# A transformer layer: the shift sums of the first products on 128 columns with idle products behind them, the first block by k-tiles, mixer casts behind the decays, and steps of the ada queue in last units

## The chip, the core and the metric

The kernel runs on one core of a Trainium2 chip. The core has TensorE (PE: products of matrices, into the banks of PSUM), VectorE (DVE), ScalarE (ACT), GpSimd (POOL) and SyncE (SP), which work through queues of their own and wait for each other by semaphores. DMA queues move data between HBM and the on-chip memory, SBUF; in this kernel SP and POOL issue them, each in its own order. The metric is the time of one execution on the device, in microseconds (us), and the median of several runs.

## The reference

One layer on 256 tokens of width 2048, in fp32, with a conditioning vector c:

```python
ada = (silu(c) @ w_ada + b_ada)
sh1, sc1, g1, sh2, sc2, g2, sh3, sc3, g3 = split(ada, 9)
modulate(x, sh, sc) = layernorm(x) * (1 + sc) + sh
h = (silu(gate) * up) @ ffn1_w_out,  gate, up = split(modulate(x, sh1, sc1) @ ffn1_w_in)
x = layernorm(ALPHA * x + 0.5 * (1 + g1) * h, ln1_g, ln1_b)
h = token_mixer(modulate(x, sh2, sc2), w_in, ...)       # 8 fox attention heads, 4 mLSTM heads
x = layernorm(ALPHA * x + (1 + g2) * h, ln2_g, ln2_b)
h = second FFN on modulate(x, sh3, sc3)
x = layernorm(ALPHA * x + 0.5 * (1 + g3) * h, ln3_g, ln3_b)
```

w_ada is 2048 x 18432, the FFN's hidden width 5632, w_in has the columns of fox q, k, v and forget gates and of mLSTM q, k, v, gates and o. So nearly all bytes are weights that are read once, and each weight meets 256 tokens.

## The kernel before

**Products.** Each fp32 product is made of three products in fp32r: a weight or a row is split into a rounded part hi (a cast, on ACT, line 150) and a rest lo (a subtraction, on DVE, line 151), and `mm3` (lines 399 to 401) adds hi x hi, lo x hi and hi x lo in PSUM. `load_w` (line 374, or 378 in parts) issues one weight unit of 1 MB on SP, into three raw buffers, and splits it in pieces of 128x1024 into six hi and six lo buffers; its argument `behind` names an instruction behind which these splits stand in the order of ACT and DVE. The order of instructions within each engine is otherwise the order in which the code issues them, with the pieces marked `pinned` or `manual_schedule` held where they are written.

**The ada vector.** `silu(c) @ w_ada` isn't made on PE but on DVE: slices of 128 rows x 1024 columns (0.5 MB) are multiplied by a column of csil and summed over k into an accumulator (lines 163 and 165). At the end of 16 slices the 128 partitions are summed by PE with a matrix of ones (`bc`, line 178, one product with ahi and one with alo), and for shifts and scales the diagonal is taken on DVE (lines 195 and 197) into `scsh`, one column per 128 features. `AdaQueue` holds these units for the whole layer: `pump(n)`, called once in each weight unit of a stage, runs a step of a finished unit's tail (casts, bc, diagonal) and then as many slices as are owed; `need(n)` runs what is missing until n units are done, and sets the debt `owed` to zero. The accumulators and slices have the names `acc`, `gate`, `ar`. In the last four units of an output's last group (`out_proj`) pump isn't called.

**The start.** Only the shifts and scales of the first 512 features (block j = 0) are needed for the first products. `first_ada0` loads the 16 slices from SP. The half of a slice that holds the scales is summed on DVE (into `gate`), the half with the shifts on PE: the `row` products (line 824), one csil column times 512 columns, into one partition of PSUM. After the sixteenth, ACT copies the row to SBUF (`shifts`, line 828), and for each k-tile of 128 features `first_columns` turns the shifts (line 789) and the scales (line 787) into columns with one-column products and adds the bias (DVE, line 791, `scsh`). `modulate_both` then writes x of that tile: ACT makes xf (line 325) and its cast xhi_f (line 328), DVE the rest xlo_f (line 331). `first_in(j, i)` makes block i of twelve for the 512 features j: 48 products of 256 columns into two PSUM tiles, all four k-tiles for one half of the columns (h = 0), then for the other; for j = 0 ACT copies the sums to `hT1a` or `hT1b` (line 894), and later rounds add to them. Between blocks `next(fa)` runs slices of the next features' sums (issued from POOL, line 850), as many as a table says.

**The mixer.** `form_a_four` makes four heads' columns of q or k (m0 and m1 for the mLSTM heads, fb and fbk for q and k of fox heads 4 to 7, then fa and fak for 0 to 3) from four weight units of 48 products each; `step()` after each unit runs work of the heads. A part of `mlstm_head`, which runs in the units of fb and fbk, is the decay of the head: PE makes gb and the two scores sps (lines 1301 and 1303), ACT Relu and Exp of the decay (lines 1306 and 1307, into `dm`), DVE masks it and multiplies it with the scores (lines 1308 and 1309). One part of the scores lies in a PSUM tile of which there is one, so the next head's scores wait until DVE has read it.

## Time and profile before

| | us |
|---|---|
| median of 3 runs | 1929.29 |
| their spread | 1928.31 to 1930.26 |
| the profiled execution | 1927.28 |
| its span | 1925.6 |
| PE busy | 1891.5 (98%) |
| DVE busy | 1483.4 (77%) |
| ACT busy | 953.7 (50%) |
| POOL busy | 59.7 (3%) |
| DMA queue of SP, share of 16 engines | 73.4% |
| DMA queue of POOL | 4.4% |

The span is what the profile shows from the first instruction to the last; the execution's own time is 1.7 longer. A row of a timeline has the start in us, the time in us, the engine, the line, the operation, out<-in, the shape, the count, and in brackets how long the engine sat idle before it and what ended that. PE's product of 256 columns is listed with its latency (0.28 us and more), and products follow each other more closely than that; an fp32 product gives two records. The granted clock is 1.00 at full rate.

### The profile page before, as it was taken

What the parts mean: (1) busy time and instruction counts of PE and PEld (TensorE: products, weight loads), DVE (VectorE), ACT (ScalarE), POOL (GpSimd) and SP (SyncE); (2) the same over time, 40 slices, a digit from 0 to 9 for tenths busy, and PEclk for the clock granted to TensorE, in tenths of its full rate; (3) what the DMA queues carried; (4) which work ended last, traced back from release to release, by engine and by line L of the source; (5) the groups of instructions that cost most, each with busy time, mean ns of one, the idle gap of its engine ahead of it and who ended that gap; (6) DMA issues with size and microseconds to landing.
All of it is one profiled execution on the core that took longest, in us unless ns stands there. A gap on an engine that the chain in (4) does not pass through costs nothing.

```text
span 1925.6 us, 32413 instructions
## 1 busy us (share of the span) xinstructions
PE 1891.5 (98%) x13133; PEld 1724.6 (90%) x13133; DVE 1483.4 (77%) x1847; ACT 953.7 (50%) x1359; POOL 59.7 (3%) x88
## 2 busy tenths in 40 slices
PE   6999999999999999999999999999999999999997
PEld 3999999999988887699989886999999999988886
...
GB/s 359 375 262 313 328 218 296 337 331 306 266 339 296 267 301 236 138 321 317 319 300 272 315 300 114 338 282 246 262 248 260 246 213 196 240 184 189 196 196 89
DMA packets 283662, 510.92 MB, mean 265 GB/s; under 512 B 10962, under 2 KB 134514, under 8 KB 282488
## 3 DMA queue, kind: packets, MB, share of 16 engines
q1 hardware_dynamic: 275640, 480.53, 73.4%
...
## 4 chain that ended last, share of the span: by engine, by line
PE 84%; DVE 7%; DMA 5%; issue 2%; ACT 1%; SPq 0%; DVEq 0%; POOL 0%; ACTq 0%
PE gu_f L401 8%; PE gu_f L400 8%; PE gu_f L399 8%; PE o_f L399 6%; PE o_f L401 6%; PE o_f L400 6%; PE s L400 4%; PE s L399 4%; PE s L401 4%; DMA ar<-in_w_ada_dram 3%; PE fs L401 1%; PE fs L399 1%; PE fs L400 1%; PE o_mx L399 1%; PE o_mx L401 1%
## 5 line engine op out<-in xcount | busy, mean ns | idle before, releaser
L165 DVE SCALAR_TENSOR_TENSOR acc<-ar,csil,acc 128x1024 f32<-128x1024 f32 (+1 forms) x167 | 211.4, 1267 | 52.2 <-DMA ar<-in_w_ada_dram 51.5
L400 PE MATMUL s<-xlo_f,hi_s 128*128 128x256 f32 x768 | 213.6, 278 | 1.2 <-DVE xlo_f L331 1.2
L399 PE MATMUL s<-xhi_f,hi_s 128*128 128x256 f32 x768 | 213.4, 279 | 0.0
L401 PE MATMUL s<-xhi_f,lo_s 128*128 128x256 f32 x768 | 213.3, 278 | 0.0
L401 PE MATMUL gu_f<-xhi_f,lo_f2i 128*128 128x256 f32 x768 | 212.0, 276 | 0.0
L399 PE MATMUL gu_f<-xhi_f,hi_f2i 128*128 128x256 f32 x768 | 212.0, 276 | 0.0
L400 PE MATMUL gu_f<-xlo_f,hi_f2i 128*128 128x256 f32 x768 | 212.0, 276 | 0.0
L151 DVE TENSOR_TENSOR lo_f2i<-raw_f2i,hi_f2i 128x1024 fp32r<-128x1024 f32 x96 | 117.4, 1224 | 92.4 <-ACT hi_f2i L150 92.4
L401 PE MATMUL gu_f<-xhi_f,lo_f1i 128*128 128x256 f32 x640 | 176.7, 276 | 0.0
L399 PE MATMUL gu_f<-xhi_f,hi_f1i 128*128 128x256 f32 x640 | 176.7, 276 | 0.0
L400 PE MATMUL gu_f<-xlo_f,hi_f1i 128*128 128x256 f32 x640 | 176.7, 276 | 0.0
L150 ACT CAST hi_f2i<-raw_f2i 128x1024 fp32r<-128x1024 f32 x96 | 100.8, 1050 | 135.4 <-PE gu_f L400 124.6
L150 ACT CAST hi_s<-raw_s 128x1024 fp32r<-128x1024 f32 x96 | 100.6, 1052 | 130.3 <-PE s L400 93.4
L400 PEld LDWEIGHTS s<-xlo_f,hi_s 128*128 128x128 f32 x768 | 145.5, 189 | 1.5 <-DVE xlo_f L331 1.5
L401 PEld LDWEIGHTS s<-xhi_f,lo_s 128*128 128x128 f32 x768 | 145.4, 189 | 0.0
L399 PEld LDWEIGHTS s<-xhi_f,hi_s 128*128 128x128 f32 x768 | 144.9, 189 | 0.0
L399 PEld LDWEIGHTS gu_f<-xhi_f,hi_f2i 128*128 128x128 f32 x768 | 144.2, 188 | 0.2
L400 PEld LDWEIGHTS gu_f<-xlo_f,hi_f2i 128*128 128x128 f32 x768 | 144.2, 188 | 0.2
L401 PEld LDWEIGHTS gu_f<-xhi_f,lo_f2i 128*128 128x128 f32 x768 | 144.2, 188 | 0.0
L151 DVE TENSOR_TENSOR lo_f2o<-raw_f2o,hi_f2o 128x1024 fp32r<-128x1024 f32 x86 | 105.2, 1223 | 43.3 <-ACT hi_f2o L150 43.3
L165 DVE SCALAR_TENSOR_TENSOR gate<-ar,csil,gate 128x1024 f32<-128x1024 f32 (+1 forms) x94 | 117.5, 1251 | 25.4 <-DMA ar<-in_w_ada_dram 25.2
L151 DVE TENSOR_TENSOR lo_s<-raw_s,hi_s 128x1024 fp32r<-128x1024 f32 x96 | 115.5, 1219 | 27.4 <-ACT hi_s L150 27.2
...
## 6 DMA issues: line engine op xcount, KB each, us to landing
ar<-in_w_ada_dram SPq DMA_DIRECT2D x227, 512.0 KB, 5.4
...
```

The lines of the kernel that those rows point to most:

```text
L150: S.copy(hi, src)
L151: return V.tensor_tensor(out=lo, in0=src, in1=hi.bitcast(F32), op=ALU.subtract)
L165: V.scalar_tensor_tensor(out=acc, in0=raw, scalar=csil[:, k:k + 1], in1=acc, op0=ALU.mult, op1=ALU.add)
L399: PE.matmul(o, ah, bh, start=start, stop=False)
L400: PE.matmul(o, ah, bl, start=False, stop=False)
L401: PE.matmul(o, al, bh, start=False, stop=stop)
```

## The change

It has six parts.

1. The `row` products take the csil column broadcast to 128 columns, so that the sum of the shifts stands in all 128 partitions of PSUM. The bias of the shifts is added there by four products of an identity column with the bias rows (`load_bcol(part)`, called at the fifth slice). In `columns0` DVE takes the diagonal of 128x128 out of PSUM into scsh; the copy of the row and the four products of the shifts are gone.
2. Idle products (128x256, fp32r, into a PSUM tile that nobody reads) are put behind rows 10 to 14 (3, 3, 3, 12, 3) and behind the first two column products (2, 2).
3. Block (0, 0) goes by k-tiles: for each k-tile both halves of the columns.
4. The first three slices of the next features (j = 1) are issued from SP, between raw_s_1 and raw_s_2, instead of from POOL, and the table of steps behind blocks 0 and 1 of j = 0 is 0, 3 instead of 2, 1; for j = 0 the casts of block i stand behind the copies of block i - 3. The three gbias loads go from SP to POOL.
5. In `form_a_four` the splits of a weight unit stand behind the Exp of a head's decay (`decays`).
6. The tail step of `pump` is a method of its own, `end_step`, which is also called in the last four units of an output's last group and behind the last two calls of `half_in` in the second FFN.

On PE, at the end of the first ada sums, stood before (row_150 is the PSUM row, gate and shifts the sums, cp and cq the columns, s_0_0 the first block's PSUM tile):

```order
L824 MATMUL row_150<-ar_0_13_214,csil 1x512
L824 MATMUL row_150<-ar_0_14_224,csil 1x512
L824 MATMUL row_150<-hT1a,csil 1x512
L789 MATMUL cp_235<-trir,shifts 128x1
L787 MATMUL cp_235<-trir,gate 128x1
L789 MATMUL cq_236<-trir,shifts 128x1
L787 MATMUL cq_236<-trir,gate 128x1
L789 MATMUL cp_235<-trir,shifts 128x1
L787 MATMUL cp_235<-trir,gate 128x1
L789 MATMUL cq_236<-trir,shifts 128x1
L787 MATMUL cq_236<-trir,gate 128x1
L399 MATMUL s_0_0_267<-xhi_f_124,hi_s_00_220 128x256
```

and stands now (row_150 is now 128 partitions, idle_151 the tile that nobody reads):

```order
L858 MATMUL row_150<-ar_0_13_227,csil 128x512
L845 MATMUL idle_151<-trir 128x256 x12
L858 MATMUL row_150<-ar_0_14_249,csil 128x512
L845 MATMUL idle_151<-trir 128x256 x3
L858 MATMUL row_150<-hT1a,csil 128x512
L816 MATMUL cp_262<-trir,gate 128x1
L845 MATMUL idle_151<-trir 128x256 x2
L816 MATMUL cq_263<-trir,gate 128x1
L845 MATMUL idle_151<-trir 128x256 x2
L816 MATMUL cp_262<-trir,gate 128x1
L816 MATMUL cq_263<-trir,gate 128x1
L405 MATMUL s_0_0_299<-xhi_f_124,hi_s_00_245 128x256
```

The four products of `shifts` are gone, and idle products stand between the rows and the columns.

On ACT, in the mixer at the change from unit group fb to fbk, where head 0's gb and the scores are made (dm is the decay of an mLSTM head, hi_fbk a weight piece's rounded part, qs the scaled q of a fox head), stood before:

```order
L150 CAST hi_fbk_10448<-raw_fbk_10446 128x1024
L150 CAST hi_fbk_10476<-raw_fbk_10446 128x1024
L150 CAST hi_fbk_10540<-raw_fbk_10538 128x1024
L150 CAST hi_fbk_10568<-raw_fbk_10538 128x1024
L1306 ACTIVATE dm_10354<-gb_10352,nacol 128x256
L1306 ACTIVATE dm_10354<-gb_10352,nacol 128x128
L1307 ACTIVATE dm_10354<-dm_10354 128x256
L1307 ACTIVATE dm_10354<-dm_10354 128x128
L150 CAST hi_fbk_10621<-raw_fbk_10619 128x1024
L1383 ACTIVATE qs_10711<-pr_fb_10121 128x256
L150 CAST hi_fbk_10649<-raw_fbk_10619 128x1024
```

and stands now:

```order
L1355 ACTIVATE dm_10398<-gb_10396,nacol 128x256
L1355 ACTIVATE dm_10398<-gb_10396,nacol 128x128
L1356 ACTIVATE dm_10398<-dm_10398 128x256
L1356 ACTIVATE dm_10398<-dm_10398 128x128
L153 CAST hi_fbk_10489<-raw_fbk_10487 128x1024
L153 CAST hi_fbk_10517<-raw_fbk_10487 128x1024
L1432 ACTIVATE qs_10752<-pr_fb_10172 128x256
L1355 ACTIVATE dm_10473<-gb_10471,nacol 128x256
L1355 ACTIVATE dm_10473<-gb_10471,nacol 128x128
L1356 ACTIVATE dm_10473<-dm_10473 128x256
L1356 ACTIVATE dm_10473<-dm_10473 128x128
L153 CAST hi_fbk_10581<-raw_fbk_10579 128x1024
```

The decay of each head (first 10398, then 10473) moved ahead of the casts of one unit, and the casts of the second unit stand behind the second head's decay.

On PE the column sums bc_3_1 of the ada queue stood before inside the second FFN's gate products (gf), with products between the one with ahi and the one with alo:

```order
L400 MATMUL gf_13839<-lo_gu_13846,xhi_f_12456 128x512
L178 MATMUL bc_3_1_13828<-ahi_3_1_13824,trir 128x512
L401 MATMUL gf_13839<-hi_gu_13845,xlo_f_12457 128x512
L399 MATMUL gf_13840<-hi_gu_13845,xhi_f_12456 128x512
L400 MATMUL gf_13840<-lo_gu_13846,xhi_f_12456 128x512
L401 MATMUL gf_13840<-hi_gu_13845,xlo_f_12457 128x512
L399 MATMUL gf_13841<-hi_gu_13845,xhi_f_12456 128x512
L400 MATMUL gf_13841<-lo_gu_13846,xhi_f_12456 128x512
L401 MATMUL gf_13841<-hi_gu_13845,xlo_f_12457 128x512
L178 MATMUL bc_3_1_13828<-alo_3_1_13825,trir 128x512
```

They stand now as a pair inside the products of fh. At the end of the mixer's output (o_mx), where no column sums stood before, there are now those of bc_2_0 and bc_2_1; yw and hi_mxo are weight pieces, y the mixer's rows:

```order
L407 MATMUL o_mx_12181<-hi_mxo_01_12306,ylo 128x512
L181 MATMUL bc_2_0_12353<-ahi_2_0_12296,trir 128x512
L181 MATMUL bc_2_0_12353<-alo_2_0_12297,trir 128x512
L405 MATMUL o_mx_12336<-yw,yh_11433 128x512
L406 MATMUL o_mx_12336<-yw_12339,yh_11433 128x512
L407 MATMUL o_mx_12336<-yw,yl_11434 128x512
L405 MATMUL o_mx_12336<-yw,yh_11433 128x512
L406 MATMUL o_mx_12336<-yw_12340,yh_11433 128x512
L407 MATMUL o_mx_12336<-yw,yl_11434 128x512
L181 MATMUL bc_2_1_12387<-ahi_2_1_12359,trir 128x512
```

The pair of bc_2_1 is pulled apart there as that of bc_3_1 was in gf: its product with alo_2_1 follows twelve products behind the one with ahi_2_1.

The diff:

```diff
@@ -108,3 +108,3 @@
-    def load_bcol():
+    def load_bcol(part):
         brow = ap.tile([72, 2, P], F32, tag="ahi", name="brow")
@@ -114,2 +114,5 @@
             PE.transpose(bps[:, i * 72:(i + 1) * 72], brow[:, i, :], ident[:72, :72])
+        for q in range(4):
+            PE.matmul(part[:, q * P:(q + 1) * P], ident[:72, q:q + 1].to_broadcast([72, P]), brow[:, 0, :],
+                      start=False, stop=False)
         V.tensor_copy(bcol.rearrange("p v k -> p (v k)"), bps[:, :144])
@@ -126,5 +129,5 @@
         SP.dma_start(hrow[5:6, :], mlstm_norm_g)
-        SP.dma_start(gbias[:, 0:8], fox_f_bias[0:1, :].to_broadcast([P, 8]))
-        SP.dma_start(gbias[:, 8:12], mlstm_i_bias[0:1, :].to_broadcast([P, 4]))
-        SP.dma_start(gbias[:, 12:16], mlstm_f_bias[0:1, :].to_broadcast([P, 4]))
+        G_.dma_start(gbias[:, 0:8], fox_f_bias[0:1, :].to_broadcast([P, 8]))
+        G_.dma_start(gbias[:, 8:12], mlstm_i_bias[0:1, :].to_broadcast([P, 4]))
+        G_.dma_start(gbias[:, 12:16], mlstm_f_bias[0:1, :].to_broadcast([P, 4]))
         yield
@@ -251,7 +254,10 @@
+        def end_step(self):
+            if self.tails:
+                with pinned():
+                    self.tail()
+
         def pump(self, n):
             self.owed += n
-            with pinned():
-                if self.tails:
-                    self.tail()
+            self.end_step()
             while self.owed >= 1:
@@ -527,2 +533,4 @@
                     npump()
+                else:
+                    ada.end_step()
             if lastg:
...
@@ -806,2 +808,29 @@
+    def columns0(acc, part, mb, ws, idle):
+        cps = aux_tile("cp0"), mm_tile("cq0")
+        diag = ap.tile([P, 2, 512], F32, tag="acc", name="diag0")[:, 0, :P]
+
+        def column(q, n):
+            cp = cps[q % 2][:, q:q + 1]
+            qs = slice(q * P, (q + 1) * P)
+            mm = PE.matmul(cp, acc[:, qs], ones[:, 0:1], start=True, stop=True)
+            idle(n, mm)
+            V.scalar_tensor_tensor(out=diag, in0=part[:, qs], scalar=1.0, in1=ident, op0=ALU.mult, op1=ALU.mult,
+                                   accum_out=scsh[:, 0, q:q + 1])
+            V.tensor_tensor(out=scsh[:, 1, q:q + 1], in0=cp, in1=bcol[:, 1, q:q + 1], op=ALU.add)
+
+        column(0, 2)
+        next(mb)
+        column(1, 2)
+        next(mb)
+        next(mb)
+        column(2, 0)
+        next(mb)
+        column(3, 0)
+        next(ws)
+        next(mb)
+        for _ in mb:
+            pass
+
+
@@ -810,4 +839,9 @@
         acc = gate[:, :512]
-        part = mm_tile("row0")
-        shifts = ap.tile([P, 2, 512], F32, tag="acc", name="shifts")[0:1, 0, :]
+        part, scratch = mm_tile("row0"), mm_tile("idle0")
+
+        def idle(n, behind):
+            with tc.issue_after(behind.ins):
+                for _ in range(n):
+                    PE.matmul(scratch[:, :T], onesr, trir, start=True, stop=True)
+
         spots = [hT[:, 4 * i:4 * i + 4, :].rearrange("p f t -> p (f t)") for i in range(KF // 4)] + [gate[:, 1024:]]
@@ -823,3 +857,6 @@
             SP.dma_start(raw, src[k * P:(k + 1) * P])
-            PE.matmul(part[0:1, :], csil[:, k:k + 1], raw[:, 0, :], start=k == 0, stop=k == KD - 1)
+            mm = PE.matmul(part, csil[:, k:k + 1].to_broadcast([P, P]), raw[:, 0, :], start=k == 0,
+                           stop=k == KD - 1)
+            if k >= 10:
+                idle((3, 3, 3, 12, 3, 0)[k - 10], mm)
             if k < KD - 1:
@@ -827,3 +864,2 @@
             else:
-                S.copy(shifts, part[0:1, :])
                 for b in range(2):
@@ -835,4 +871,6 @@
                 next(mb)
+            if k == 4:
+                load_bcol(part)
             yield
-        first_columns(0, acc, mb, ws, shifts)
+        columns0(acc, part, mb, ws, idle)
         yield
@@ -849,3 +887,3 @@
             raw = where.tile([P, 2, 512], F32, tag=tag, bufs=n, name=f"ar0_{j}_{k}")
-            G_.dma_start(raw, src[k * P:(k + 1) * P])
+            (SP if j == 1 and k < 3 else G_).dma_start(raw, src[k * P:(k + 1) * P])
             if k < KD - 1:
...
@@ -876,5 +914,7 @@
         for k, hi, lo in load_w(W1[j * 512:(j + 1) * 512, c0:c0 + 512], 4, 512, f"s{j}_{i}",
-                                not i + j):
+                                not i + j, behind=None if j else copied.get(i - 3)):
             yield 4 * j + k, hi, lo
+    copied = {}
+
     def first_in(j, i, ws):
@@ -882,9 +922,16 @@
         pss = [mm_tile(f"s{j}_{i}_{b}") for b in range(2)]
+        def one(h, k, hi, lo, start, stop):
+            for b, ps in enumerate(pss):
+                fs = slice((2 * b + h) * P, (2 * b + h + 1) * P)
+                mm3(ps[:, h * T:(h + 1) * T], hi[:, fs], lo[:, fs], xT[0][:, k, :], xT[1][:, k, :], start, stop)
+
         ws = list(ws)
-        for h in range(2):
-            for k, hi, lo in ws:
-                for b, ps in enumerate(pss):
-                    fs = slice((2 * b + h) * P, (2 * b + h + 1) * P)
-                    mm3(ps[:, h * T:(h + 1) * T], hi[:, fs], lo[:, fs], xT[0][:, k, :], xT[1][:, k, :],
-                        k == 4 * j, k == 4 * j + 3)
+        if i + j == 0:
+            for w in ws:
+                for h in range(2):
+                    one(h, *w, w[0] + h == 0, w[0] + h == 4)
+        else:
+            for h in range(2):
+                for w in ws:
+                    one(h, *w, w[0] == 4 * j, w[0] == 4 * j + 3)
         for b, ps in enumerate(pss):
@@ -893,3 +940,3 @@
             if j == 0:
-                S.copy(part, ps)
+                copied[i] = S.copy(part, ps).ins
             else:
@@ -924,4 +971,2 @@
         next(fa)
-        if k == 4:
-            load_bcol()
     with tc.manual_schedule(engines={mybir.EngineType.DVE, mybir.EngineType.Activation}):
@@ -947,3 +992,4 @@
                 first_in(j, i, ws if i + j == 0 else first_w(j, i))
-            for _ in range((2, 1, 2, 1, 2, 2, 1, 2, 1, 2, 1, 0)[i] if j < 3 else i not in (4, 9, 11)):
+            for _ in range((2 * (j > 0), 1 + 2 * (j == 0), 2, 1, 2, 2, 1, 2, 1, 2, 1, 0)[i] if j < 3
+                           else i not in (4, 9, 11)):
                 with pinned():
@@ -1072,2 +1118,3 @@
     emptied = [None]
+    decays = [None, None]
@@ -1115,3 +1162,4 @@
                 before_last()
-            for k4, hi, lo in load_w(W[u * 512:(u + 1) * 512, c0:c0 + 512], 4, 512, f"{name}{u}"):
+            for k4, hi, lo in load_w(W[u * 512:(u + 1) * 512, c0:c0 + 512], 4, 512, f"{name}{u}",
+                                     behind=decays[0]):
                 k = 4 * u + k4
@@ -1121,2 +1169,3 @@
                         k + f % 2 == 0, k + f % 2 == KD)
+            decays[:] = decays[1], None
             step()
@@ -1306,3 +1355,3 @@
             S.activation(d, gb[:, i * P:T], AF.Relu, bias=nacol[:, i, h:h + 1])
-            S.activation(d, d, AF.Exp, scale=-1.0)
+            decays[1] = S.activation(d, d, AF.Exp, scale=-1.0).ins
             V.tensor_tensor(out=d[:, :P], in0=d[:, :P], in1=triu1[:, :P], op=ALU.mult)
@@ -1517,2 +1566,4 @@
         ps = half_in(j, 0, "fh")
+        if j >= 8:
+            ada.end_step()
         for f in range(2):
```

12 lines of the change are left out of this document (3 added, 9 removed).

## The prediction

> **What bounds the kernel now.** I read the page's busy times first, then the waits of TensorE (PE), then the granted clock window by window, then the timeline at the two places that these show. First the page:
>
> ```profile
> PE 1891.5 (98%) x13133; PEld 1724.6 (90%) x13133; DVE 1483.4 (77%) x1847; ACT 953.7 (50%) x1359; POOL 59.7 (3%) x88
> ```
>
> PE is busy for 98% of the span, so only what PE waits for, and what it does at half clock, can be won. The waits of PE that bear on this change (total us, times, longest):
>
> ```profile
> PE sps L1303 <- DVE dm L1309: 4.1, 1, 4.1
> PE bc L178 <- DVE alo L151: 1.5, 2, 0.9
> PE s L400 <- DVE xlo_f L331: 1.2, 1, 1.2
> PE bc L178 <- ACT ahi L150: 0.5, 1, 0.5
> ```
>
> The windows around the first products (after the window: its length, then busy time and count of PE, PEld, DVE, ACT and POOL, then granted clock, DMA share, GB/s), and two in the mixer:
>
> ```profile
> 29.51:32.92 3.41, 1.90 (x4) 0.17 (x4) 2.51 (x4) 0.83 (x1) 0.66 (x2) 1.00 1.05 390
> 32.92:36.34 3.42, 2.76 (x19) 2.51 (x19) 1.07 (x5) 2.15 (x5) 0.62 (x1) 1.00 1.03 387
> 36.34:39.75 3.41, 2.22 (x10) 1.93 (x10) 1.96 (x4) 2.58 (x5) 0.00 (x0) 0.50 1.04 386
> 39.75:43.16 3.41, 3.41 (x18) 3.41 (x17) 2.88 (x4) 2.37 (x4) 0.72 (x1) 0.50 1.04 381
> 43.16:46.57 3.41, 3.41 (x32) 3.41 (x31) 3.41 (x4) 2.81 (x4) 0.96 (x2) 1.00 1.07 343
> ```
>
> ```profile
> 971.61:975.02 3.41, 0.66 (x4) 0.61 (x5) 3.41 (x9) 1.61 (x3) 0.00 (x0) 1.00 0.99 365
> 975.02:978.43 3.41, 3.41 (x19) 3.41 (x18) 3.41 (x4) 1.51 (x5) 0.00 (x0) 0.50 1.05 401
> ```
>
> The first block runs at half clock from 36.34 to 43.16, behind a window whose PE time is almost all one-column products. The mixer loses its clock for one window behind one with 0.66 us of work. A window with 1.90 us of row products (29.51) kept it.
>
> **The start.** PE's rows:
>
> ```profile
> 32.03 1.02 PE L824 MATMUL row<-hT1a,csil 128*1 128x512 f32 x2 [0.30 <-DMA hT1a<-in_w_ada_dram]
> 33.72 0.38 PE L789 MATMUL cp<-trir,shifts 1*128 1x1 f32 x2 [0.66 <-ACT shifts L828]
> 36.13 0.60 PE L399 MATMUL s<-xhi_f,hi_s 128*128 128x256 f32 x2
> 42.14 0.41 PE L401 MATMUL s<-xhi_f,lo_s 128*128 128x256 f32 x1
> 42.35 0.41 PE L400 MATMUL s<-xlo_f,hi_s 128*128 128x256 f32 x1
> 45.61 0.28 PE L401 MATMUL s<-xhi_f,lo_s 128*128 128x256 f32 x1
> 45.73 0.28 PE L399 MATMUL s<-xhi_f,hi_s 128*128 128x256 f32 x1
> 51.17 0.28 PE L399 MATMUL s<-xhi_f,hi_s 128*128 128x256 f32 x1
> ```
>
> Block 1 takes 51.17 - 45.73 = 5.44 us for 48 products, 0.113 each; at half clock they are 42.35 - 42.14 = 0.21 apart. Block 0 takes 45.73 - 36.13 = 9.6 us, so 4.16 us too many: 1.2 of it is the wait for xlo_f, the rest the clock. What stands ahead of it on DVE and ACT:
>
> ```profile
> 32.30 0.88 DVE L165 SCALAR_TENSOR_TENSOR gate<-hT1a,csil,gate 128x256 f32<-128x256 f32 x2
> 34.45 0.16 DVE L791 TENSOR_TENSOR scsh<-cp,bcol 128x2 f32<-128x2 f32 x1 [1.27 <-PE cp L787]
> 35.74 0.42 DVE L331 TENSOR_TENSOR xlo_f<-xf,xhi_f 128x256 fp32r<-128x256 f32 x1 [0.51 <-ACT xhi_f L328]
> 37.58 1.23 DVE L151 TENSOR_TENSOR lo_s<-raw_s,hi_s 128x1024 fp32r<-128x1024 f32 x1 [1.35 <-ACT hi_s L150]
> 33.09 0.57 ACT L828 COPY shifts<-row 1x512 f32<-1x512 f32 x1 [2.75 <-PE row L824]
> 34.70 0.56 ACT L325 ACTIVATE xf<-tp,scsh 128x256 f32<-128x256 f32 x1 [1.04 <-DVE scsh L791]
> ```
>
> Before, the chain is last row (33.05), copy 33.09 + 0.57, column products from 33.72, scsh at 34.45, xf at 34.70, first product at 36.13, when the eighth column product leaves PE. The copy goes, and with it four of the eight. A column product then needs only the last sum on DVE (32.30 + 0.88 = 33.18). The diagonal on DVE is new: 128x128 out of PSUM with a sum. It lies between the 0.16 of a 128x2 row and the 0.42 of a 128x256 one; I take 0.3, and one 0.16 add. So scsh at about 33.8, xf at 33.9, and with the same 1.43 from xf to the first product that starts at 35.2 to 35.3: 0.9 us earlier, 0.5 to 1.3 with the bounds.
>
> By k-tiles, the first 24 products need only the first half of the weights, 24 x 0.113 = 2.7 us of PE, to 38.0. In that time lo_s of the second half, now behind the second xlo_f, must end: the row at 37.58 moved forward by 0.9 ends at 37.9. The wait of 1.2 shrinks to what ACT's xf (0.56) and its cast leave: about 0.5, between 0 and 1.2. If the clock holds, block 0 ends at 35.25 + 5.44 + 0.5 = 41.2, against 45.73: 4.5 won. If it falls as before for two windows, some 32 products (6.82 us at 0.21) cost 0.1 more each, 3.2 us, and 1.3 is won. Does it hold? The window ahead of the first product would have some 1.1 us of full-rate products plus the four idle ones behind the columns (0.45) and four column products, where before it had only column products. That is 1.55 us and the columns, next to the 1.90 that kept the clock and the 0.66 that lost it: nearer to the first. I take that it holds. The rows themselves ride behind their slices, of 0.52 MB each, 1.34 us apart at the 390 GB/s of that window (their 512 columns move as before, 1.02 for the pair of records); the idle products of 3 x 0.113 and 12 x 0.113 fit behind them, and only the 3 behind the fifteenth row (0.34) stand close to the last row, which waited 0.30 for DMA: 0 to 0.1 of cost.
>
> [...]
>
> Behind block 0 the weights must follow. Block 2's first cast waited for its DMA, block 4's too:
>
> ```profile
> 43.76 2.00 ACT L150 CAST hi_s<-raw_s 128x1024 fp32r<-128x1024 f32 x2 [1.61 <-DMA raw_s<-in_ffn_w_in_dram]
> 55.03 2.00 ACT L150 CAST hi_s<-raw_s 128x1024 fp32r<-128x1024 f32 x2 [2.93 <-DMA raw_s<-in_ffn_w_in_dram]
> ```
>
> Block 2 will start at about 41.2 + 5.44 = 46.6; its casts end at 45.8 and its first lo_s (1.23) at about 46.1 to 47. Three ada slices are now ahead of raw_s_2 on SP instead of on POOL: the same bytes ahead of it, so it lands no later, but no sooner. Block 4 starts at 57.5; its second lo_s ends at about 58.5, and is wanted 24 products in, at 60.2. I charge 0.5 of stalls, 0 to 3. Start: 4.5 - 0.5 = 4.0 won, between 0 and 5.4 (1.3 earlier, and all of the 4.16).
>
> **The mixer.** PE, then ACT and DVE:
>
> ```profile
> 964.26 0.38 PE L1303 MATMUL gb<-o 128*128 128x128 f32 x2
> 969.98 0.28 PE L1301 MATMUL gb<-ng,rowsel 128*128 128x256 f32 x1
> 974.36 0.70 PE L1303 MATMUL sps<-o 128*128 128x256 f32 x2 [4.10 <-DVE dm L1309]
> 966.32 2.00 ACT L150 CAST hi_fbk<-raw_fbk 128x1024 fp32r<-128x1024 f32 x2 [1.94 <-DMA raw_fbk<-in_w_in_dram]
> 968.23 0.72 ACT L1306 ACTIVATE dm<-gb,nacol 128x256 f32<-128x256 f32 x2
> 968.84 0.61 ACT L1307 ACTIVATE dm<-dm 128x256 f32<-128x256 f32 x2
> 967.61 1.28 DVE L165 SCALAR_TENSOR_TENSOR acc<-ar,csil,acc 128x1024 f32<-128x1024 f32 x1 [0.69 <-DMA ar<-in_w_ada_dram]
> 973.89 0.41 DVE L1309 TENSOR_TENSOR dm<-sps,dm 128x256 f32<-128x256 f32 x1
> ```
>
> Head 0's gb is done at 964.7, but ACT first casts two more fbk units, one of them 1.94 late by DMA, and only then does Relu and Exp (968.23 to 969.45). On DVE the dm stands behind four lo casts, so the second head's sps waits for the shared PSUM tile until 974.36. With the casts behind the decays, Relu and Exp run at 964.7 to 966.0. DVE's dm (the 0.41 of the row at 973.89 and three smaller, about 1 us) then stands behind three running sums of 1.28 of ada slices, which the new order takes earlier, rather than behind casts: it ends between 967 and 971, against the 970.1 at which sps is wanted. So 4.1 goes, or 3 of it; take 3.6. The half-rate window goes with it (a wait of 1 us leaves 2.4 us of work in a window): 16 products at 0.1, and the sps at half rate, 1.7. What is late next are the casts: hi_fbk at 966.0 to 968.0 and its lo's to about 970, wanted at 970.9; the second unit's stand behind head 1's decays (gb 970.6, decays to 971.9, casts to 973.9, lo's and a sum to 976 to 977.5), wanted at 976.3 and 977.7. I charge 0.5, 0 to 3. Mixer: 3.6 + 1.7 - 0.5 = 4.8 won, between 1.5 and 5.8.
>
> **The ada queue.** Its column products (bc) leave the gate products for fh, and fh for the end of the mixer's output, where the casts they need are only just made, as at the end of the first FFN's output, whose 0.5 and 0.9 stay:
>
> ```profile
> 1300.41 0.50 PE L178 MATMUL bc<-alo,trir 128*128 128x512 f32 x1 [0.60 <-DVE alo L151]
> 1220.00:1230.00 10.00, 10.00 (x89) 9.91 (x88) 10.00 (x11) 6.85 (x13) 0.00 (x0) 1.00 1.07 356
> 1218.75 2.00 ACT L150 CAST hi_fh<-raw_fh 128x1024 fp32r<-128x1024 f32 x2 [5.58 <-DMA raw_fh<-in_ffn_w_in_dram]
> 1223.92 0.28 PE L399 MATMUL fh<-xhi_f,hi_fh 128*128 128x256 f32 x1
> ```
>
> The 0.6 goes; the like of 0.5 + 0.9 comes (0 to 1.7): 0.8 lost. No slice is added, but up to three more of 0.52 MB run ahead of fh's weights at 356 GB/s, 1.47 us each. The cast of 1218.75 is done 3.2 before its product at 1223.92; a unit three slices later would be 4.4 late, one slice later 1.5. I charge 0, and keep 2 for the range. The bias rows (4 products on PE), the three gbias loads on POOL instead of SP and the end steps in the last units stand behind slices or products that PE does anyway: nothing, 0.3 at most.
>
> **The sum** is 4.0 + 4.8 - 0.8 = 8.0 us off the profiled execution of 1927.28 (span 1925.6), so 1919.3. The median of the runs, 1929.29, stands 2.0 above that execution: 1921.3.
>
> **The rivals.**
> First, the clock falls at the start all the same: the start wins 1.3 - 0.5 = 0.8, and the time is 1929.3 - 4.8 + 0.8 - 0.8 = 1924.5. The 1.55 us of work against 1.90 speaks for it, the four columns beside it against.
> Second, the change gives its gain back to DMA: block 0 ends early but blocks 2 to 5 stand for their weights (3 instead of the 0.5 charged), and fh for 2: 1921.3 + 2.5 + 2 = 1925.8, about no change. For it: a DMA share of 1.03 to 1.07 in both places; against it: the same bytes in the same order.
> Third, slower: casts behind decays come late in each of the four fbk units. A wait of over 2.5 us in a unit empties most of a window, as at 971.61, and costs 1.7 for the half-rate one behind it: 4 x (2.5 + 1.7) = 16.8 lost for 5.8 won, so 1929.3 - 4.0 + 0.8 + 11.0 = 1937. It decides where the lo's of the second unit end after 979 rather than 976 to 977.5, that is where DMA makes the sums ahead of them wait 2 us rather than the 0.69 of the row at 967.61.
> That the change does not do what it says: the ends of FFN1 are one such place (its 0.5 and 0.9 stay), and it is in the sum.
>
> **Chances and range.** The forecast 0.60, with a range of its own from 1916.5 (all best ends, 5.4 + 5.8 + 0.6, and 1.0 for the spread of the runs, 1928.31 to 1930.26) to 1924; the first rival 0.17, the second 0.13, the third 0.10. Less than 0.2% (3.9 us) is about what a measurement of this kernel can't tell from no change: faster is under 1925.4, slower over 1933.2. The forecast, 0.13 of the first rival and 0.04 of the second make 0.77 faster; the rest of these two makes 0.13 the same; the third is 0.10 slower. The range 1916.5 to 1928 leaves out the third and some 0.08 at the ends of the others.
>
> **What would show it.** In the profile after: the clock at 1.00 in every window from 30 to 47; first product at about 35.3 and block 1 at 41.2; no PE wait for xlo_f over 0.6; no sps wait over 1 and no half-rate window near 970; a bc wait at the end of o_mx. A DMA wait of PE's weights in blocks 2 to 5 or in fh, or casts of fbk that end after PE asks for them, would make it wrong.

## The result, and the profile after

The changed kernel takes 1940.41 us (six runs, 1939.6 to 1941.29), the kernel before in runs on the same chip 1929.56 (1926.91 to 1933.45). The ratio is 1.0055, with a 95% interval from 1.0042 to 1.0068: some 11 us slower. The prediction was 1921.3, some 8 faster. The span of the profiled execution is 1937.9, against 1925.6.

The waits of PE after the change (total us, times, longest):

```profile
PE row L858 <- DMA hT1a<-in_w_ada_dram: 10.1, 3, 9.5
PE bc L181 <- DVE alo L154: 4.2, 1, 4.2
PE pr_m L407 <- DVE lo_m L154: 3.5, 3, 2.1
PE pr_fb L407 <- DVE lo_fb L154: 2.0, 1, 2.0
PE b_mv L406 <- DVE lo_mv L154: 1.9, 3, 1.2
```

The wait for sps, 4.1 before, is gone from this list. In its place stand waits for lo casts of the mixer's weights (b_mv are the products of the mLSTM heads' v, pr_m and pr_fb those of the units m and fb of `form_a_four`: 7.4 together), and a bc wait of 4.2. To see where the time goes, the start of the same piece of work is compared in both traces (us in the span; the last two columns are the stretch from the first product of b_mv, near the beginning of the mixer, to the first of the second FFN's products into fs, and the span):

| | first row | first product | block 1 | first of j = 1 | b_mv | fbk | fs | b_mv to fs | span |
|---|---|---|---|---|---|---|---|---|---|
| before | 10.13 | 36.13 | 45.73 | 108.36 | 854.61 | 975.07 | 1309.83 | 455.2 | 1925.6 |
| after | 12.33 | 38.04 | 44.13 | 108.72 | 853.12 | 979.16 | 1322.16 | 469.0 | 1937.9 |

Block 1 starts 1.6 earlier, not 4.5; 64 us later, at the first product of j = 1, that is lost again. In part that is this one execution: six kernels of the experiments below (e2, e3, e4, e6, e7 and e9) have the same instructions up to there, and come to their first product at 36.95 to 37.29 and to j = 1 at 106.72 to 107.15, 1.2 to 1.6 ahead of before. At the beginning of the mixer the kernel is 1.5 ahead. From there to fs it loses 13.8, and nothing changes behind it.

The start, PE's rows after the change:

```profile
12.33 4.83 PE L858 MATMUL row<-hT1a,csil 128*128 128x512 f32 x6 [9.47 <-DMA hT1a<-in_w_ada_dram]
36.32 0.29 PE L816 MATMUL cp<-trir,gate 128*128 128x1 f32 x2
38.04 0.50 PE L405 MATMUL s<-xhi_f,hi_s 128*128 128x256 f32 x2 [0.28 <-ACT xhi_f L334]
```

The first row waits 9.47 for its slice, and begins 2.2 later than before (12.33 against 10.13). The rows behind it come one slice after another, and the first product comes at 38.04, 2.8 later than forecast. Block 0 takes 44.13 - 38.04 = 6.09. What arrives while the first slices are awaited, before and then after (two us of the span; the last three figures are the granted clock, the DMA share and GB/s):

```profile
6.00:8.00 2.00, 0.00 (x0) 0.00 (x0) 1.83 (x4) 0.00 (x0) 0.00 (x0) 1.00 1.00 421
```

```profile
6.00:8.00 2.00, 0.00 (x0) 0.00 (x0) 1.82 (x4) 0.00 (x0) 0.00 (x0) 1.00 1.14 170
```

The DMA engines are as busy as before, and move 170 GB/s in place of 421. What POOL now issues first stands in its timeline:

```profile
1.84 0.71 POOL L130 DMA_DIRECT2D gbias<-in_fox_f_bias_dram  x1
2.54 0.54 POOL L131 DMA_DIRECT2D gbias<-in_mlstm_i_bias_dram  x1
```

These two write 12 values of 4 bytes into each of 128 partitions, in pieces of 32 and 16 bytes, and together only 6 KB. The third gbias load, again of 16 bytes per partition, is issued at 9.88, behind this window.

The mixer, in the window in which the time goes, before and after:

```profile
840.00:975.00 135.00, 130.90 (x1019) 125.47 (x1018) 119.19 (x165) 77.32 (x125) 1.13 (x2) 1.00 0.94 323
```

```profile
840.00:975.00 135.00, 127.64 (x972) 120.42 (x971) 115.27 (x157) 69.87 (x118) 1.12 (x2) 1.00 0.91 313
```

PE, DVE and ACT all do less, and DMA moves less, too. So the loss is neither more bytes nor more work of an engine. What SP issues in it, after:

```profile
852.35 0.46 SPq L380 DMA_DIRECT2D raw_mv<-in_w_in_dram  x1
855.93 2.18 SPq L187 DMA_DIRECT2D ar<-in_w_ada_dram  x2
858.16 0.46 SPq L380 DMA_DIRECT2D raw_mv<-in_w_in_dram  x1
...
889.92 2.16 SPq L187 DMA_DIRECT2D ar<-in_w_ada_dram  x2
892.13 0.46 SPq L380 DMA_DIRECT2D raw_m<-in_w_in_dram  x1
```

and before:

```profile
851.78 0.47 SPq L374 DMA_DIRECT2D raw_mv<-in_w_in_dram  x1
...
862.00 0.37 SPq L184 DMA_DIRECT2D ar<-in_w_ada_dram  x1
862.46 0.42 SPq L374 DMA_DIRECT2D raw_mv<-in_w_in_dram  x1
...
883.05 0.37 SPq L374 DMA_DIRECT2D raw_m<-in_w_in_dram  x1
```

After the change each weight unit has a pair of ada slices (x2) ahead of it, and six units take 892.13 - 852.35 = 39.8 us, 6.6 each. Before, some units have one slice or none, and six take 883.05 - 851.78 = 31.3, 5.2 each. The slices (tile ar, from 840 to 950 us, after) show where 6.6 comes from:

```profile
L168 DVE SCALAR_TENSOR_TENSOR gate<-ar,csil,gate x15: 1269/1279/1286, 869.6 to 921.8; 128x1024 f32<-128x1024 f32 x15
DMA to landing us min/median/max: 4.1/5.3/6.2
```

There are two slice buffers. One is free again after the slice has landed (5.3) and DVE has summed it (1.28), which is 6.6 together. A pair per unit needs both buffers once per unit, and the unit's own load stands behind the pair in SP's queue. Without the lead (e2 below) PE goes through the eight units of b_mv in 47.9 us, 6.0 each with the small products between them, and a unit of m, of 48 products, keeps it for 5.4 (48 x 0.113). So PE, with weights every 6.6, has to wait. SP's waits for slices to land and ACT's waits for the weights of m, from 840 to 975 us, before and then after (total, times, longest), go the same way:

```profile
SPq L184 <- DMA ar<-in_w_ada_dram: 22.0, 15, 3.8
ACT hi_m L150 <- DMA raw_m<-in_w_in_dram: 11.0, 5, 2.7
```

```profile
SPq L187 <- DMA ar<-in_w_ada_dram: 35.8, 22, 3.1
ACT hi_m L153 <- DMA raw_m<-in_w_in_dram: 19.4, 6, 5.9
```

Why are there pairs? Counted in the traces over both queues, 170 ada slices are issued ahead of the first unit of b_mv in both kernels, but 186 after the change and 181 before it ahead of the first unit of m (the expectations below give 128 and 123, with the same five between them). The three slices of j = 1 that moved from POOL to SP are no part of these five, since both queues are counted. The five hang on `need`, which is called between the first FFN and the mixer, and which sets the debt to zero only inside its loop:

```python
def need(self, n):
    while self.done < n:
        self.owed = 0
        ...
```

Before, the sixth unit's tail still had steps to do at need(6), and so the debt of slices was set to zero there. With end steps in the last units of the first FFN's output the sixth unit is done by then, the loop doesn't run, and the debt stays. From then on `pump` issues slices earlier than before: five more stand ahead of the first unit of m, two to four ahead of fb, fbk and fa, none ahead of the first unit of fh, and four again ahead of fs. The reason is so far read from the code; the experiments test it.

### The profile page after: what moved, and what is told of

It reads as the page before. It is cut to its first block, busy times and chain, and to the rows that moved or that the text cites. A ratio compares the mean times of both kernels' runs of the same rounds, so it can differ in the third digit from the quotient of the medians.

```text
span 1937.9 us, 32457 instructions
## 1 busy us (share of the span) xinstructions
PE 1896.5 (98%) x13161; PEld 1731.0 (89%) x13161; DVE 1483.8 (77%) x1855; ACT 948.1 (49%) x1358; POOL 60.1 (3%) x88
## 4 chain that ended last, share of the span: by engine, by line
PE 77%; DMA 12%; DVE 6%; ACT 2%; issue 2%; SPq 0%; DVEq 0%; POOL 0%; ACTq 0%
PE gu_f L405 8%; PE gu_f L407 8%; PE gu_f L406 8%; PE o_f L405 8%; PE o_f L407 8%; PE o_f L406 8%; DMA ar<-in_w_ada_dram 4%; PE s L405 4%; PE s L406 4%; PE s L407 4%; DMA raw_fh<-in_ffn_w_in_dram 3%; DMA raw_s<-in_ffn_w_in_dram 2%; PE fs L406 1%; PE fs L407 1%; PE fs L405 1%
```

## The experiments

My theory at this point: the lead of the queue costs the time from b_mv to fs, and the gbias loads cost the start. The rivals: the end steps' own work (their casts and column sums) costs it; the casts behind the decays do (the third rival of the prediction); or the queue of SP holds weights up merely by standing in order.

**The gbias loads.** Back to SP, with all else as changed (e1_gbias_sp), and the same without part 6 (e5_gbias_sp_no_end):

```diff
-        G_.dma_start(gbias[:, 0:8], fox_f_bias[0:1, :].to_broadcast([P, 8]))
-        G_.dma_start(gbias[:, 8:12], mlstm_i_bias[0:1, :].to_broadcast([P, 4]))
-        G_.dma_start(gbias[:, 12:16], mlstm_f_bias[0:1, :].to_broadcast([P, 4]))
+        SP.dma_start(gbias[:, 0:8], fox_f_bias[0:1, :].to_broadcast([P, 8]))
+        SP.dma_start(gbias[:, 8:12], mlstm_i_bias[0:1, :].to_broadcast([P, 4]))
+        SP.dma_start(gbias[:, 12:16], mlstm_f_bias[0:1, :].to_broadcast([P, 4]))
```

> The changed kernel, with the three gbias loads back on SP's queue. The first row product came at 12.33 us in the changed kernel against 10.13 before, and the DMA rate fell to 50 to 130 GB/s for about 1.6 us at 6 to 8 us, just when POOL's small loads ran. Theory A (POOL's packets of 16 and 32 bytes hold up the first slices): the first row at about 10.1 and the time about 2.2 below the changed kernel's 1940.4, so 1938.2, faster than it by 1.5 to 2.5. Rival (the first slice landed late for another reason, or the weights are short behind it anyway): first row at 12.3, or earlier but with the gain lost by 108 us, and 1940 to 1941.

Measured: 1941.68, ratio to before 1.0072 [1.0057, 1.0087], no better than the change. But the first row comes at 10.23, the first product at 34.93 and block 1 at 41.02: 4.7 earlier than before. The start is what the prediction said, once these loads are out of its way. By j = 1 the kernel is at 107.84, only 0.5 ahead of the kernel before.

> Both: gbias back on SP and no end steps. If A and B hold and add up, 2.2 below the kernel without the end steps: 1918 to 1923, which is faster than the kernel before. If the start's advance is lost to late weights before 108 us, the same as the kernel without the end steps.

Measured: 1924.7, 0.9982 [0.997, 0.9995]. Block 1 is at 40.93, j = 1 at 108.32. The wait that takes the lead back, and its window:

```profile
PE cp L790 <- DVE scsh L792: 1.4, 1, 1.4
```

```profile
100.00:110.00 10.00, 8.88 (x63) 8.88 (x64) 5.18 (x11) 7.38 (x15) 0.00 (x0) 0.83 0.63 211
```

At the end of the sums for j = 1, PE waits, and behind it the clock falls for one window (0.83 on average in these 10 us). The wait shown is 1.4 and 16 products at half rate cost 1.7, 3.1 together; it is in both kernels with these loads on SP. With the loads of gbias in the first FFN instead (e13_bias_loads_in_ffn1, part 6 left out as in e5):

```diff
+    pin["h1"] = pin["h"]
     npool.release()
...
         need(6)
+        with tc.issue_after(pin["h1"]):
+            V.memset(gbias, 0.0)
+        SP.dma_start(gbias[:, 0:8], fox_f_bias[0:1, :].to_broadcast([P, 8]))
+        SP.dma_start(gbias[:, 8:12], mlstm_i_bias[0:1, :].to_broadcast([P, 4]))
+        SP.dma_start(gbias[:, 12:16], mlstm_f_bias[0:1, :].to_broadcast([P, 4]))
```

> The changed kernel without end steps, with the gbias loads in the first FFN (behind a small write of 16 columns that comes after the first products, so that they can't go earlier), and every buffer at its old address. Theory I (the small packets cost the DMA some 2 us wherever it is the bound): first row at 10.1, block 1 at 41, j = 1 at 105 to 106, and 2 faster than without end steps: 1919 to 1921. Rival J (the bytes alone bound the first 108 us): block 1 at 41, j = 1 at 106.8 or later, 1921 to 1924.

Measured: 1920.25, 0.9948 [0.993, 0.9967], the best median of all kernels here, below both the kernel before and the changed one; its interval overlaps that of the same kernel with these loads on POOL (e2 below). The first row is at 10.03, block 1 at 40.82, and j = 1 at 104.68, so 3.7 of the lead are kept there:

```profile
100.00:110.00 10.00, 10.00 (x89) 10.00 (x89) 5.15 (x9) 7.85 (x14) 0.00 (x0) 1.00 0.61 199
```

**The lead.** Part 6 left out, so that need(6) zeroes the debt again (e2_no_end_steps); the whole change with the debt set to zero by hand, the end steps kept (e4_debt_zero); and part 6 left out, with a debt of four slices put in by hand (e7_lead_of_four):

```diff
# e2: both calls of end_step
-                else:
-                    ada.end_step()
...
-        if j >= 8:
-            ada.end_step()
# e4, on the changed kernel
         need(6)
+        ada.owed = 0
# e7, on e2
         need(6)
+        ada.owed = 4
```

> The changed kernel without the calls of the end step (neither in the last units of an output nor behind the last calls for fh). The debt of the ada queue is then set to zero again by need(6), and the slices stand as before the change: 119 of them ahead of the seventh mv unit rather than 120, 123 rather than 128 ahead of m. Theory B (the queue runs 2 to 5 slices ahead, and the weights and lo's behind its slices come late): the waits of PE in mv, m and fb (about 10 us with the clock), in fa (3), in fh (2) and the one of 4.2 behind alo with its half-rate window (5 to 6) go, the 1.7 at the end of the first FFN's output comes back, and the time is 1920 to 1925. Rival C (decays ahead of the casts make the casts late): the waits in mv, m, fb and fa stay, and the time is 1933 to 1938.

> The changed kernel with the end steps, but with the debt of the ada queue set to zero behind need(6). Theory B (it is the lead that costs): the waits in mv, m, fb and fa go as without the end steps, and the first FFN's output keeps its gain of 1.7, so 1920 to 1928, above the lower end only as far as the column sums that the end steps move (end of the mixer's output, fh) wait on their own. Rival D (the end steps cost by where they put their casts and sums, whatever the lead): the waits in mv to fa stay and the time is 1932 to 1940.

> The changed kernel without end steps, but with a debt of four slices set behind need(6), which puts the slices where the changed kernel has them (128 ahead of m, 144 ahead of fbk, 194 at the fourth pair of fh, against 123, 142 and 190). Theory B (the lead alone costs): the waits in mv to fa come back, some 11 to 15 us over the 1922.1 without end steps: 1932 to 1938. If it takes the end steps too: 1922 to 1926.

| | median | ratio to before | b_mv to fs |
|---|---|---|---|
| before | 1929.56 | 1 | 455.2 |
| after | 1940.41 | 1.0055 [1.0042, 1.0068] | 469.0 |
| e2, no end steps | 1922.09 | 0.9969 [0.9958, 0.998] | 451.3 |
| e4, end steps, no debt | 1923.08 | 0.9973 [0.996, 0.9985] | 454.0 |
| e7, no end steps, lead | 1934.47 | 1.0029 [1.0017, 1.004] | 463.0 |

Each ratio is to the kernel before on the same chip, where its median lies between 1928.14 and 1929.56. The last column is of one profiled execution each, which stands off its kernel's median by -0.8 (after), -0.7 (e2), 1.6 (e4) and 2.6 (e7).

One line that sets a number to zero takes 17 us off the changed kernel (e4; 16 by the ratios), though all six parts are in it. And a lead alone, without a single end step, costs 12 (e7 against e2). The counts of slices follow: 181 ahead of the first unit of m in e2 and e4, 186 in e7. What SP issues, first in e2 and then in e7, differs as it did between before and after:

```profile
856.88 0.46 SPq L380 DMA_DIRECT2D raw_mv<-in_w_in_dram  x1
860.43 0.37 SPq L187 DMA_DIRECT2D ar<-in_w_ada_dram  x1
860.89 0.42 SPq L380 DMA_DIRECT2D raw_mv<-in_w_in_dram  x1
...
881.07 0.37 SPq L380 DMA_DIRECT2D raw_m<-in_w_in_dram  x1
```

```profile
855.00 0.46 SPq L380 DMA_DIRECT2D raw_mv<-in_w_in_dram  x1
858.57 2.38 SPq L187 DMA_DIRECT2D ar<-in_w_ada_dram  x2
861.00 0.46 SPq L380 DMA_DIRECT2D raw_mv<-in_w_in_dram  x1
...
888.85 0.46 SPq L380 DMA_DIRECT2D raw_mv<-in_w_in_dram  x1
```

In e2 the five units from 856.88 to 881.07 take 4.8 each; in e7 the five from 855.00 to 888.85 take 6.8 each, with pairs. From 840 to 975 us SP waits 22.8 for slices to land in e2 and 32.5 in e7, ACT 11.8 and 19.0 for the weights of m. PE's wait for lo_mv is back:

```profile
PE b_mv L406 <- DVE lo_mv L154: 3.9, 1, 3.9
```

The window from 840 to 975 us agrees, e2 first (PE busy for 134.66 of 135), then e7:

```profile
840.00:975.00 135.00, 134.66 (x1051) 129.02 (x1050) 118.03 (x166) 75.89 (x127) 1.12 (x2) 1.00 0.93 317
```

```profile
840.00:975.00 135.00, 127.53 (x966) 120.60 (x965) 117.53 (x161) 69.72 (x115) 1.12 (x2) 0.99 0.91 310
```

**Order in the queue or buffers?** If the weights were late only because they stand behind waiting slices on SP, slices issued from POOL would cure it (e6_slices_from_pool). If the cycle of two buffers bounds it, smaller slices in more buffers shorten the cycle (e10_half_slices: each slice as two halves of 512 columns, in a ring of four half buffers of the same total size, each half summed and freed alone). Both stand on the changed kernel:

```diff
# e6
+    pool_rows = []
...
-            SP.dma_start(raw, src[k * P:(k + 1) * P])
+            (G_ if pool_rows else SP).dma_start(raw, src[k * P:(k + 1) * P])
...
         need(6)
+        pool_rows.append(True)
# e10 (the other places that use these buffers are left out here)
+    ring, turn_h = ap.tile([P, 4, 512], F32, tag="araw", name="aring"), [0]
...
-            raw = ap.tile(list(acc.shape), F32, tag="araw", bufs=2, name=f"ar{tag}_{k}")
-            SP.dma_start(raw, src[k * P:(k + 1) * P])
-            ada_acc(acc, raw, k)
+            for v in range(2):
+                vs = v if len(acc.shape) == 3 else slice(v * 512, (v + 1) * 512)
+                raw = ring[:, turn_h[0] % 4, :]
+                turn_h[0] += 1
+                SP.dma_start(raw, src[k * P:(k + 1) * P, vs])
+                ada_acc(acc[:, vs], raw, k)
```

> The changed kernel, lead and end steps kept, but behind need(6) the ada slices are issued from POOL's queue, so that a slice that waits for its buffer holds up no weight unit on SP. In the changed kernel SP waited from 840 to 975 us for 36 us on slices' DMA and 47 us on DVE's sums before it could issue a slice, against 22 and 38 before, while the DMA share was 0.91 and not above before's. Theory E (the lead costs because SP stands at a slice's buffer with the weights behind it): the waits in mv, m, fb and fa go or shrink to a third, and the time is 1922 to 1931. Rival F (the lead costs because the slices' bytes take the DMA's time or DVE's order, whoever issues them): the waits stay and the time is 1937 to 1942, or longer, since POOL needs 0.7 us for an issue.

Measured: 1964.72, 1.0182 [1.0155, 1.0209], 24 us slower still. SP's weights are free, but the slices now come late, and DVE stands in order with the lo casts behind their sums (waits of DVE, 840 to 1000 us, then one of PE):

```profile
DVE acc L168 <- DMA ar<-in_w_ada_dram: 16.4, 11, 4.0
```

```profile
PE b_fv L408 <- DVE lo_fv L154: 8.3, 5, 3.3
```

So it is not SP's order alone: the wait only moved to the next queue in which slices and weights meet. The test is not a clean one, since an issue on POOL takes 0.65 us (median), on SP 0.37, and 9.3 of the loss are there before b_mv begins.

> The changed kernel, lead and end steps kept, but a slice comes as two halves of 512 columns in a ring of four half buffers (the same 8 KB per partition), each half summed and its buffer freed by itself. In the changed kernel a pair of slices and the next weight unit left SP every 6.6 us in mv (852.35 to 892.13 us, six units), which is the slices' landing of 5.3 and DVE's sum of 1.28, while PE takes a mv unit in 5.8. Theory G (two slice buffers bound the weights behind them whenever a unit carries two slices): a pair now cycles in about 5, the waits in mv, m, fb and fa shrink by most of their 11, and the time is 1928 to 1934, with the wait of 4.2 at alo left. Rival F (the slices' bytes or DVE's time bound it): 1939 to 1943, since DVE's halves cost some 0.1 each and SP issues twice as often.

Measured: 1931.72, 1.0013 [0.9998, 1.0028]: 8.7 of the loss comes back with the lead untouched. The halves land sooner:

```profile
DMA to landing us min/median/max: 2.7/4.4/7.1
```

The six units from 848.89 to 886.46 take 6.3 each, next to 6.6. The cycle got shorter, by less than the landing alone promises; SP's waits for slices to land, from 840 to 975 us, fell from 35.8 to 15.3, and the stretch from b_mv to fs to 458.4 (in an execution 4.3 below the median, the fastest of ten, so most show more). Where there is no lead, halves should not help, and they don't: e2 with halves (e14_half_slices_no_end) takes 1924.6, 0.9979 [0.9968, 0.9991], and e13 with halves (e15_both) 1923.13, 0.9966 [0.9954, 0.9977], neither better than without. For e15 1917 to 1920 was expected, so that is a miss. A third slice buffer of full size, the direct test of the cycle, was not run: that the two buffers set the 6.6 is argued from landing and sum, and borne out by the halves.

> The changed kernel without end steps, with half slices in a ring of four half buffers. If the two slice buffers hold up weights without the lead too (in fh and at the wait for sps): 1 to 3 below 1922. If they only matter with the lead: 1922 to 1923.

> Both of these: gbias loads in the first FFN and half slices, no end steps. If both theories hold: 1917 to 1920, below both the kernel before and the changed one.

**The parts on their own.** The decays alone, on the kernel before (e8_decays_alone); the start alone, the changed kernel without parts 5 and 6 (e9_no_end_no_decays); and e2 without the idle products (e12_no_idle_products):

```diff
# e8
+    decays = [None, None]
...
-            for k4, hi, lo in load_w(W[u * 512:(u + 1) * 512, c0:c0 + 512], 4, 512, f"{name}{u}"):
+            for k4, hi, lo in load_w(W[u * 512:(u + 1) * 512, c0:c0 + 512], 4, 512, f"{name}{u}", behind=decays[0]):
...
+            decays[:] = decays[1], None
...
-            S.activation(d, d, AF.Exp, scale=-1.0)
+            decays[1] = S.activation(d, d, AF.Exp, scale=-1.0).ins
# e9, on e2: the argument behind=decays[0] left out
# e12, on e2
-                for _ in range(n):
+                for _ in range(0):
                     PE.matmul(scratch[:, :T], onesr, trir, start=True, stop=True)
```

> The kernel before with part 5 alone (the splits of a unit behind the decay of a head). Theory (the wait for sps of 4.1 and the half-rate window of 1.7 go, the casts still come in time): 4 to 6 faster than the kernel before, ratio 0.9970 to 0.9980. Rival C (the casts come late): 0 to 3 faster or slower.

Measured: 1924.62, 0.9974 [0.9963, 0.9985], so 5 us faster than before. What is left of the wait of 4.1:

```profile
PE sps L1305 <- DVE dm L1311: 0.5, 1, 0.5
```

> The changed kernel without end steps and without part 5: parts 1 to 4 alone, which is the start. By the profiles the start is 4.1 ahead at block 1 (counted from the first row) and 1.5 to 2 ahead from j = 1 on: 1.0 to 2.5 faster than the kernel before, 1926 to 1927; the 4.1 would stay whole (1924) only if the weights of blocks 2 to 12 kept pace.

Measured: 1927.89, 0.9998 [0.9985, 1.0011]: with gbias on POOL the start alone is no gain. It is 1.3 ahead at j = 1 (107.08), and the sps wait, here 6.4 in an execution 4.2 above the median, is longer than before:

```profile
PE sps L1349 <- DVE dm L1355: 6.4, 1, 6.4
```

> The changed kernel without end steps and without the idle products (the tile they write is never read, so nothing of the result is left out). Theory (the idle products hold the clock): a window or two at half rate in block 0, which takes 7.5 to 9.5 us rather than 6.1; of these 1.4 to 3.4 us some is taken back at j = 1, where the weights bound: 1922 to 1925. Rival (the 128 columns and the earlier first product hold it anyway): block 0 takes 6.1 to 6.5 and the time is as without end steps.

Measured: 1924.33, 0.9983 [0.9969, 0.9996], 2.2 above e2, with intervals that overlap; j = 1 comes at 111.58, where e2 has 106.83. The windows of 3.41 us around the first products:

```profile
31.19:34.60 3.41, 1.62 (x4) 0.30 (x2) 1.80 (x3) 1.04 (x1) 0.00 (x0) 1.00 1.05 388
34.60:38.01 3.41, 3.38 (x10) 2.35 (x10) 1.93 (x9) 0.77 (x2) 0.00 (x0) 0.50 1.04 385
38.01:41.42 3.41, 3.35 (x15) 3.26 (x16) 2.73 (x10) 3.35 (x7) 0.00 (x0) 0.50 1.05 386
```

Without idle products two windows run at half rate (0.50) behind one with 1.62 us of PE time, as two did in the kernel before behind one with 2.76. The slice isn't much later: in the first of these windows a row waits 1.59 for its slice and begins at 33.28; in e2 it begins at 33.02, and twelve idle products stand where the wait is, so that 30.80 to 34.20 shows 3.23 us of PE time there and the clock stays at 1.00. In the seven windows from 24.00 to 47.80 us it is 1.00 in e2, in e13 and in the changed kernel. So it held with the idle products and fell without them, in the one execution of e12 that was profiled, which is the slowest of ten, 7.3 above the median.

**What is left of the loss.** The changed kernel is 6 us above e7. Its wait of 4.2 at the end of fh, and the half-rate window behind it:

```profile
1302.87 0.52 PE L181 MATMUL bc<-alo,trir 128*128 128x512 f32 x1 [4.20 <-DVE alo L154]
```

```profile
1303.00:1306.00 3.00, 3.00 (x15) 2.96 (x16) 3.00 (x5) 0.00 (x0) 0.54 (x1) 0.54 0.75 226
```

would account for 4.2 + 1.7 = 5.9. So the end step behind fh alone was left out (e3_no_fh_end_step):

```diff
         ps = half_in(j, 0, "fh")
-        if j >= 8:
-            ada.end_step()
```

> The changed kernel without the end step behind the last two calls for fh; the lead and the end steps of the outputs stay. Theory H (the end step brings the tail's column sum one weight unit nearer to its casts, so PE stands 4.2 at the product with alo and loses a window's clock): that wait and the window go, 4 to 6 faster than the changed kernel, 1934 to 1937. Rival (the wait comes from the lead, the sums being late on DVE): it stays, 1939 to 1941.

Measured: 1940.75, 1.0068 [1.0049, 1.0086], not faster. In its profiled execution the 4.2 is gone:

```profile
PE bc L181 <- DVE alo L154: 1.4, 2, 0.8
PE fh L407 <- DVE lo_fh L154: 2.0, 2, 1.2
```

The wait for lo_fh grew from 1.0 to 2.0, and the way from b_mv to fs takes 467.3 against 469.0. This execution ran in 1937.5, 3.2 under the median, so it may show less of such waits than most do. The account of 5.9 was therefore wrong as a price of that one step, and what makes up the 6 us stays open. The lead itself isn't larger: the changed kernel and e7 have the same count of slices ahead of m (186) and of fbk (202), and e7 has one more ahead of fb, fa and fs. In the profiled executions 4.9 of the 6 lie in fh, which lasts to the first product of gf: 97.2 in the changed kernel, 92.3 in e7. In e3 it is 92.6, so the step does cost there; but e3's execution loses 2.7 more than the changed kernel's between b_mv and fh (362.6 against 359.9), and in the median nothing is won. With no lead the end steps cost 1.0 (e4 against e2), with intervals that overlap.

**An accident.** Two kernels were 39 us and more slower than e2, for a reason that has nothing to do with the change. In e11_bias_loads_late gbias was taken from the constants and put into the mixer's own memory; e16_64_bytes has e2's instructions and in addition an unused tile of 64 bytes per partition among the constants (and one memset for it):

```diff
# e11, on e2 (the three loads follow the new tile, on SP)
-    gbias = cst.tile([P, 16], F32, name="gbias")
...
+    gbias = mx.tile([P, 16], F32, name="gbias")
...
# e16, on e2
+    pad = cst.tile([P, 16], F32, name="pad")
+    G_.memset(pad, 0.0)
```

> The changed kernel without end steps, with the three gbias loads neither in the first 10 us (POOL, as changed) nor at 39 us (SP, as before) but in the mixer, ahead of the fv units. On POOL they put the first row 2.0 to 2.2 later; on SP the first row came at 10.1 and block 1 was 4.7 ahead, but nothing was left at j = 1, behind a wait for the column sums and a half-rate window. Theory I (the small packets cost the DMA 2 us wherever the DMA is the bound): the first row at 10.1, block 1 at 41, j = 1 at 105 to 106.5, 2 to 3 ahead of before; time 1918 to 1921 against 1922 without end steps. Rival J (the first 108 us are bound by the bytes alone): j = 1 at 107 or later, time 1921 to 1924.

> The changed kernel without end steps, with 64 bytes of padding per partition among the constants, so that all that lies behind moves by 64 bytes. If the offset alone slows the products, they come 0.117 to 0.120 apart and the time is about 1960; if not, 0.113 and 1922, and the slow run with the loads in the mixer has another cause.

Measured: 1965.51, 1.0193 [1.0175, 1.0211], and 1961.04 in a single run. What moved, by the sizes of the tiles in the code, is the address of everything behind the constants, by 64 bytes, down in one case and up in the other. Products of the first FFN in e2, and then in e16 (both from PE's timeline, with one product of each of two lines between):

```profile
400.09 0.28 PE L405 MATMUL gu_f<-xhi_f,hi_f1i 128*128 128x256 f32 x1
...
400.43 0.28 PE L405 MATMUL gu_f<-xhi_f,hi_f1i 128*128 128x256 f32 x1
```

```profile
400.17 0.28 PE L407 MATMUL gu_f<-xhi_f,hi_f1i 128*128 128x256 f32 x1
...
400.53 0.28 PE L407 MATMUL gu_f<-xhi_f,hi_f1i 128*128 128x256 f32 x1
```

Three products take 0.34 in the one and 0.36 in the other. That is why e13 keeps gbias where it was, and gives it a memset, so that its loads stand in the first FFN.

## Why the prediction was wrong

**What failed.** The step on the ada queue. It said "No slice is added, but up to three more of 0.52 MB run ahead of fh's weights", charged 0 and kept 2 for the range. Three things in it were wrong. The lead was taken as three slices at most; it was five ahead of m, as the end steps stop `need` from clearing the debt, a line that the diff doesn't touch. Its place was taken to be fh; ahead of the first unit of fh there is no lead, but it stands in the mixer before that, where 7.4 of PE's waits are, and again in fh. And its price was reckoned as bytes, 1.47 us per slice at 356 GB/s, from which it seemed hidden; measured, a lead of this kind costs 12 (e7 against e2), and with the end steps 17 (e4 against the changed kernel). The traces point to the slice buffers: two of them turn a pair in 6.6, and a unit lasts 5.4 to 6.0 on PE. The prediction named the end steps "nothing, 0.3 at most". Their own work is 1.0 (e4 against e2), within the spread of the runs; what they do to the debt is the loss.

**The second rival** came nearest: the gain is given back, and fh waits. But it looked for a DMA share of 1.03 to 1.07, and the share fell from 0.94 to 0.91 where the time was lost. **The third**, casts behind decays that come late, did not happen: e8 wins 5 with just that part.

**The gbias loads** were in the same "nothing, 0.3 at most". They hold the first row back by 2.2 (it comes at 12.33, with these loads elsewhere at 10.13 before, 10.23 in e1 and 10.03 in e13), more than half of the 4.0 claimed for the start, and the start alone (e9) brings nothing that can be measured. From 6 to 8 us DMA moves 170 GB/s at a share of 1.14 after the change, 100 to 150 at 1.01 to 1.16 in e2, e3, e4, e7 and e10, which have these loads on POOL too, and 399 at 0.95 in e13, which has them in the first FFN. Whether the small pieces or the issue from POOL make the difference no run here shows.

**The start** was right in mechanism, and at block 1 in size: 41.2 was forecast, 41.02 and 40.82 are measured without these loads (e1, e13). Block 0 was to take 5.44 and 0.5; it takes 6.09. Of the 4.5 won there, 0.5 was charged for supply behind it; with gbias on SP, 4.2 are lost by j = 1 (e1: 4.7 ahead at block 1, 0.5 at j = 1). Only 0.7 of that is a wait for weights (lo_s). More is a wait for the next features' sums (1.1) with a half-rate window behind it (1.7), which the prediction left out. In e13, 3.7 stay at j = 1. It is 2.1 ahead of e2 there, and its median is 1.8 lower, but the intervals of the two overlap, and in its profiled execution the lead doesn't last: the first product of j = 2 comes at 172.92 (e2 174.84), that of j = 3 at 244.26 (e2 243.26), behind a wait of 1.4 for the next sums. So it isn't shown that the start's gain reaches the end.

**The clock** at the start, the first rival, held as forecast: the window ahead of the first product's (32.72 to 36.14) shows 3.26 us of PE time at a clock of 1.00, where 1.55 and the columns were reckoned. Whether 1.55 would have held it, as 1.90 did in the kernel before, was the author's estimate, and with 3.26 in its place the run does not test it. PE time alone does not sort the windows of these traces: the rate fell behind windows with 1.62 us (e12, in one execution), 2.76 and 0.66 (the kernel before), and held behind one with 1.90.

**The mixer** was right: 4.8 forecast, 5 measured (e8).

**The bc waits** were forecast as 0.8 lost, with the 0.5 and 0.9 at the end of the first FFN staying. They went: the end steps reach that place too, and b_mv is 1.5 earlier. What came instead is the 4.2 at the end of fh.

Without part 6 the change takes 1922.09 (e2), 6.0 off by its ratio where 8.0 were forecast for the whole. That is near, but not quite for the reasons given: 2.2 of the start is missing there.
